# One hybrid encoder layer on one core: the block inverses and the batches behind them written as two streams, and the fill of projections spread evenly

## The chip, the cores and the metric

The kernel runs on one core of one Trainium2 chip. A core has a matrix engine (TensorE, "PE" in the profile, its weight loads "PEld"), three engines for elementwise work (VectorE "DVE", ScalarE "ACT", GpSimd "POOL"), and SyncE ("SP"), which here issues the DMAs. Each engine works through a queue of its own in order, and semaphores make one wait for another. The metric is the time of one execution in microseconds (us) on the device; lower is better.

## The reference

One layer is computed for two groups of frames that share all weights: 64 frames of a running stream and 512 frames of a new one, 576 columns together, with a width of 1024 and 16 heads of 64.

```python
h   = RMSNorm_pre_mix(x)
p   = h @ w_in           # [r|k|v|lora_w|lora_a|lora_g] | [u|v] | gate_A | gate_B
o_A = RWKV-7 time mixing # per token: S = S*w + (S a) b^T + v k^T ;  y = S r
o_B = u * (tril(W_s) LN(v) + b)
m   = sigmoid(gate_A) * (o_A @ w_proj_a) + sigmoid(gate_B) * (o_B @ w_proj_b)
x   = x + RMSNorm_post_mix(m @ w_o)
x   = x + RMSNorm_post_ffn((silu(f @ w_gate) * (f @ w_up)) @ w_down),  f = RMSNorm_pre_ffn(x)
```

The outputs are both groups' `y`, the last projected rows, the states `S`, and the normalised `v` rows of the running stream.

## The kernel before

Activations are kept transposed, with channels on the partitions and 576 columns in two halves of 288. A large product is done in blocks of 128 output channels. Each weight block (512 KB) is loaded into `raw`, split by ScalarE and GpSimd into a high and a low part (`whi`, `wlo`), and multiplied in 48 matmuls (8 pieces of the contraction, 3 products, 2 halves). In the stage in question these matmuls are named `pj`, and `gv` for the gMLP's `v`.

The RWKV stage goes over 8 pairs of heads. The recurrence is done in chunks of 64 tokens, nine per pair, and each chunk needs the inverse of a triangular 64 x 64 matrix. Per pair there are these pieces, each a Python generator:

- `elementwise`: two low-rank products (`z`), the decays (`L`, `EL`), the squared keys `q` and their norms (matmul `n`), then the inner products in the chunks (`am`, giving `AB` and `AK`), three transposes (`tb`), the values (`tv`, `wv`) and a bonus term (`bo`). Its `am` products are marked done by the signal `("A", pair)`, all of it by `("elem", pair)`.
- `inverse`: diagonal 16 x 16 blocks of `AB` go to DRAM (`d_inv`) and come back regrouped as `M`. VectorE inverts them in 15 steps of two instructions (lines 854 and 857, `Xt` and `X`). The result `X` goes to DRAM and comes back as `IV`. VectorE transposes it (`IT<-IV`, line 865), TensorE grows the inverse to 32 and 64 rows in four small products (`m` twice, `mp`, `mu`), with a second transpose between them. Then comes, in the same generator, what is here called the batch: the products `d`, `e` and `c` over all chunks at once, VectorE's sums of them (`TD`, line 944), and `y`.
- `chain`: the state steps over the chunks, one `pc` matmul and one VectorE sum `S` (line 983) each, then the state's part of the output (`py`).
- `finish`: the group norm (`gm`, `gq`), a transpose (`to`), the gate product (`g`), and the store to `d_oa`.

The order of TensorE's instructions is fixed when the program is recorded. A class `Weave` keeps an estimated clock: each generator yields a time or a signal that it waits for, the first ready one in the list records its next instructions, and where none is ready a few matmuls of the next projection block are recorded instead. `LAT` is the table of the estimated waits, and the numbers that `ps1` gets are estimated holds of a PSUM bank. `FILL` says how many blocks of other projections (gates and `u`) are placed behind the three projection blocks (`k`, `r`, `v`) that the next pair needs. Blocks that `FILL` doesn't name run behind the last pair's chain, ahead of the output products `pa`. The other engines' queues are ordered by a scheduler, by its own estimate of when each instruction can run.

One list names all generators in their order of precedence:

```python
clk.run(chain_all(), fin_all(), inv_all(), elem_all(), norm1(0), norm1(1), ...)
```

Of the kernel before, what the change touches and what calls it, by code (L numbers as in the profile page):

```python
# [12 lines left out]
P = 128  # L13
# [7 lines left out]
NPAIR = NH // 2  # L21
# [13 lines left out]
UPR = 0  # L35
F0 = 3
OAE = (0, 0, 0, 0, 0, 0, 0, 0)
FILL = (1, 0, 2, 5, 3, 3, 1, 2)
LAT = {
# [4 lines left out]

# [1 line left out]
}  # L46


# [186 lines left out]
def layer(tc, I, O):  # L235
# [27 lines left out]
    def ps1(name, hold=0.0):  # L263
        clk.take(hold)
        return psum.tile([P, 512], F32, tag="a", bufs=nb["a"], name=name)
# [387 lines left out]
    def elementwise(E):  # L653
# [72 lines left out]
        E["AB"] = AB  # L726
        maskb = mask.unsqueeze(1).broadcast_to([P, 4, P])
        inner = lambda pm, rows_, rows, x, c: mmul(pm[rows_].rearrange("p (a t) -> p a t", t=64), BK[rows, x, c * 64:(c + 1) * 64], AR[rows, :, c * 64:(c + 1) * 64], start=True, stop=True)
        banks = lambda: [ps1("am", 3.0).rearrange("p (j t) -> p j t", t=P) for _ in range(2)]
        yield from clk.free(4)  # L730
        pm = banks()
        for c, j, half_ in PLACES2[:8]:
# [95 lines left out]
        yield LAT["bo0"]  # L828
        for hs in HS:
            yield from clk.free()  # L830
            sb = ps1("bo", 1.2)
            mmul(sb[:, 0:HALF], bonesr, rkh[:, hs], start=True, stop=False)
            mmul(sb[:, 0:HALF], bonesr, rkl[:, hs], start=False, stop=True)
            dve.tensor_tensor(bonus[:, hs], sb[:, 0:HALF], v[:, hs], ALU.mult)
            yield LAT["bo"]
# [2 lines left out]


    def inverse(E):  # L840


        hp_, AB, di = E["hp"], E["AB"], d_inv[E["hp"]]
        M = rp.tile([P, SB, SB], F32, tag="M", name="M")[0:NU]
# [20 lines left out]
        turn = lambda: dve.transpose(IT.rearrange("p c t -> p (c t)"), IV.rearrange("p c t -> p (c t)"))  # L865
        U = AB.rearrange("p j h t -> p (j h) t")
        yield lat("U", hp_)

        PT = rp.tile([P, 10, SB], F32, tag="PT16", name="PT16")
        turn()  # L870
# [31 lines left out]
                mmul(pp[a1:a1 + 32, u], IV[a1:a1 + 32, u, 32:64], PT[a1:a1 + 32, u, :], start=True, stop=True)  # L902
        for _, a1 in blocks:
            act.activation(IT[a1:a1 + 32, :, 0:32], pp[a1:a1 + 32], ACT.Copy)

        yield (("tb", hp_), 0.0)
        yield lat("d0", hp_)
        At, Kt, Vt, AR, AK, WV = (E[n] for n in ("At", "Kt", "Vt", "AR", "AK", "WV"))
        yield from clk.free(3)
        pp = [ps1("d", 2.8).rearrange("p (u t) -> p u t", t=P) for _ in range(3)]  # L910
        for c, b in CROSS:
# [2 lines left out]
                mmul(pp[b][HR[half_], 2 * (j % 2) + h], IT[HR[half2], 2 * j2 + h, :], AB[HR[half2], j2, h, 64:192], start=True, stop=True)  # L914
        for b, rows, j0, j1 in ((0, slice(0, P), 0, 2), (1, slice(0, P), 2, 4), (2, HR[1], 4, 5)):
            act.activation(AB[rows, j0:j1, :, 0:P].rearrange("p j h t -> p (j h) t"), pp[b][rows, 0:2 * (j1 - j0)], ACT.Copy)
        yield LAT["e0"]
        yield (("values", hp_), 0.0)
        if hp_ > 0:
            yield (("chain", hp_ - 1), 0.0)  # L920

# [121 lines left out]
    def elem_all():  # L1043
        for p_ in range(NPAIR):
            if p_ > 0:
                yield (("elem", p_ - 1), 0.0)
            yield from elementwise(EV[p_])
        sp.dma_start(O["shift"], shc)
        e_es.close()
        R["g"], R["gp"] = mk("gmlp")  # L1050
        R["vn"] = [slot(j) for j in range(5)]
        clk.signal("vn")
        R["ln"] = [slot(5 + i) for i in range(2)]
        R["tril"] = R["gp"].tile([P, P], F32, name="tril")
        sp.dma_start(R["tril"], I["cst"][:, NCST:])
        for i in range(2):
            sp.dma_start(R["ln"][i][0:64], I["rows"][i:i + 1, :].broadcast_to([64, D]))

    def inv_all():
        for p_ in range(NPAIR):  # L1060
            yield (("A", p_), 0.0)
            yield from inverse(EV[p_])

    def chain_all():
        for p_ in range(NPAIR):
            yield (("inv", p_), LAT["ch0"])
            yield from chain(EV[p_])

    def fin_all():
        for p_ in range(NPAIR):  # L1070
            yield (("chain", p_), 0.0)
            yield from finish(EV[p_])
# [11 lines left out]
    def oa_all():  # L1084

        yield (("chain", NPAIR - 1), 0.0)
        r_es.close()
        R["m"], R["mp"] = mk("merge")
        raw = []
        wide = lambda n: R["mp"].tile([P, D], F32, tag=n, bufs=1, name=n)  # L1090

        def load(j):
            raw.append(wide(("bias", "wsT")[j - 2])[:, 0:T] if j in (2, 3) else mixed(("gin", "", "zb", "xt")[j // 2], bufs=2))
            sp.dma_start(raw[j], d_oa[j])

        def cut(j):
            keepers(oas, split(R["mp"], raw[j], f"m{j}", eng=(dve, pool)[OAE[j]]))

        for j in range(NPAIR - 1):
            load(j)  # L1100
        yield LAT["oa"]
        for j in range(NPAIR - 1):
            cut(j)
            if j == 3:
                R["bias"], R["wsT"] = wide("bias"), wide("wsT")
                sp.dma_start(R["bias"], I["rows"][2:3, :].broadcast_to([P, D]))
                sp.dma_start(R["wsT"].rearrange("p (g t) -> p g t", t=P), I["wsT"])
            yield LAT["oaj"]
        clk.signal("mp")
        yield (("oa", NPAIR - 1), 0.0)  # L1110
        load(NPAIR - 1)
        yield LAT["oa"]
        cut(NPAIR - 1)
        yield (("behind",), 0.0)
        r2_es.close()
        l_es.close()
        h_es.close()
        R["d0"], R["dp0"] = mk("hidden0", side="right")
        R["x"], R["xf"] = mk("xf", side="right")
        R["f"], R["fp"] = mk("ffnin", side="right")  # L1120
        R["m2"], R["map"] = mk("merge2")
        clk.signal("xf")
# [159 lines left out]
    def norm1(h):  # L1282
        hs = HS[h]
        yield (("po", h), LAT["rs"])
        b = yield from rstd_row(R["fp"], R["acc1"], STARTS[h], "r1")
        keep = tc.keep_in_program_order
        fh, fl = fs
        for j in range(10):
            if j < 8:
                keep(dve.tensor_tensor(y[j][:, hs], y[j][:, hs], b, ALU.mult))  # L1290
            if 1 <= j < 9:
                i = j - 1
                keep(dve.tensor_tensor(y[i][:, hs], y[i][:, hs], xt[i][:, hs], ALU.add))
                act.activation(fh[i][:, hs], y[i][:, hs], ACT.Copy, scale=V("g_pre_ffn", i))
            if j > 1:
                i = j - 2
                keep(dve.scalar_tensor_tensor(fl[i][:, hs], y[i][:, hs], V("g_pre_ffn", i), f(fh[i][:, hs]), ALU.mult, ALU.subtract))
                fcount[h] = i + 1
            yield LAT["f0"] if j == 0 else LAT["f"]
        clk.signal("y", h)  # L1300

    def norm2(h):
        hs = HS[h]
        yield (("y", h), 0.0)
        for j in range(8):
            square_sum(mix_q, R["acc2"], y[j][:, hs], j == 0, hs, pool)
            yield LAT["sq"]
        yield LAT["rs"]
        b = yield from rstd_row(R["fp"], R["acc2"], STARTS[h], "r2")
        act.activation(R["rs2"][:, hs], b, ACT.Copy)  # L1310
        clk.signal("rs2", h)
# [21 lines left out]
    def hidden():  # L1333

        yield (("y", 1), 0.0)
        for h in range(2):
            for j in range(NF):
                yield (("fp", h, j), 0.0)
                yield (("rs2", h), 0.0)
                swiglu(j, {h: halfway[h, j]}, HS[h], pin=True)  # L1340
                clk.signal("d", h, j)
        for j in range(8):
            sp.dma_start(d_x1[j], y[j])
        R["m2"].close()
        R["m"].close()
        R["g"].close()
        R["d"], dp = mk("hidden")
        for j in range(NF, NFF):
            for x, n in zip(ds, "hl"):
                x.append(dp.tile([P, T], F32R, name=f"d{j}{n}"))  # L1350
        clk.signal("hidden")
# [127 lines left out]
    with tc.manual_schedule(engines={mybir.EngineType.PE}):  # L1479
        lora = {0: lora_w(lora_raw(0), pin=False)}  # L1480
        for nm, b in (("k", BLK_K), ("r", BLK_R), ("v", BLK_V)):
            take = Shifted(b, nm, scale=True)
            EV[0][nm] = [take(h, raw0[nm][:, HS[h]]) for h in range(2)][1]
            clk.signal(nm, 0)
        clk.run(chain_all(), fin_all(), inv_all(), elem_all(), norm1(0), norm1(1), norm2(0), norm2(1), hidden(), oa_all(), ob_all(),
                ln_all(), norm3(0), norm3(1))
    R["o"].close()
    R["d0"].close()
# [19 lines left out]
```

## Time and profile before

| | |
|---|---|
| runs shown | 1254.59, 1257.19, 1259.83 us (median 1257.19) |
| profiled execution | 1257.89 us, of which the program's span is 1256.1 |
| mean granted TensorE clock | 0.977 of full speed |
| recurrent stage with its fill | from about 63 us (first `z`) to about 640 us (first `pa`) |

The page of the profile gives the busy time of each engine, then the span in 40 slices, each digit the busy share in tenths. `PEclk` is the clock granted to TensorE, in tenths. The view by stretches gives, for each, its length, the busy time of PE, PEld, DVE, ACT and POOL with the number of instructions, the mean clock, and the share and rate of the DMAs. The view of waits says which engine's instruction waited for which. A row of a time line has start, length, engine, line, operation, output and inputs, shape, count, and in brackets the idle time of the engine ahead of it with what ended it. A row of the chain of work that ended last has start, length and name alone. The trace counts two matmul records for each matmul of full-precision operands, so the counts there are up to twice those of the program.

### The profile page before, as it was taken

How to read it: one execution, taken by the hardware profiler on the slowest of the kernel's cores; microseconds unless marked ns; L12 is line 12 of the kernel's file. 1: busy time of each engine (PE TensorE's matmuls, PEld its weight loads, DVE VectorE, ACT ScalarE, POOL GpSimd, SP SyncE). 2: the span in 40 equal slices, each digit the busy share in tenths (PEclk: the TensorE clock that was granted, in tenths of full speed). 3: DMA queues.
4: the chain of work that ended last, by engine and by line, in shares of the span. 5: the costliest groups of instructions: out<-in, count | busy, mean ns of one | idle time of the engine just before them, and what ended most of it. 6: DMA issues, size and time to landing. Idle time of an engine off the chain costs nothing.

```text
span 1256.1 us, 29917 instructions
## 1 busy us (share of the span) xinstructions
PE 1194.0 (95%) x12926; PEld 1159.7 (92%) x12926; DVE 545.3 (43%) x1081; ACT 464.7 (37%) x889; POOL 621.2 (49%) x484
## 2 busy tenths in 40 slices
PE   6999999998979898889999999899999999999997
PEld 6989999998978898889999999899999999999997
DVE  5756473737364646552803441654333333300003
ACT  5545354544343435333531233443222222222220
POOL 6654454545344544531634554465656556543442
PEclk8989999998989999999999999999999999999998
DMA  5232222222212221221544653232222222243222
GB/s 181 81 97 91 78 87 77 87 78 56 84 49 63 76 76 49 82 74 53 171 161 142 200 156 101 68 110 84 77 80 81 84 85 85 81 156 93 76 77 76
DMA packets 68276, 118.05 MB, mean 94 GB/s; under 512 B 30832, under 2 KB 36208, under 8 KB 68144
## 3 DMA queue, kind: packets, MB, share of 16 engines
q1 hardware_dynamic: 68000, 116.06, 30.0%
q8 instruction: 101, 1.65, 0.5%
q14 instruction: 31, 0.25, 0.1%
q10 hardware_dynamic: 144, 0.08, 0.0%
HBM read 99.83 MB, written 16.28 MB: 92 GB/s over the span
## 4 chain that ended last, share of the span: by engine, by line
PE 75%; DVE 12%; issue 3%; DMA 3%; ACT 3%; POOL 2%; SPq 1%; DVEq 0%; ACTq 0%; POOLq 0%
PE fg L287 20%; PE pj L287 16%; PE po L287 15%; PE pb L287 4%; PE pa L287 4%; PE gv L287 3%; DVE Xt L854 2%; DVE X L857 2%; PE am L287 1%; PE z L287 1%; PE y L287 1%; PE d L287 1%; SPq L862 1%; PE c L287 1%; PE n L287 1%
## 5 line engine op out<-in xcount | busy, mean ns | idle before, releaser
L306 POOL TENSOR_TENSOR wlo<-raw,whi 128x512 fp32r<-128x512 f32 (+1 forms) x288 | 401.7, 1418 | 397.2 <-ACT whi L303 350.1
L303 ACT ACTIVATE whi<-raw 128x1024 fp32r<-128x1024 f32 x144 | 150.2, 1047 | 287.2 <-PE fg L287 174.2
L1259 DVE TENSOR_TENSOR rs<-rs,nsq 128x288 f32<-128x288 f32 (+2 forms) x12 | 9.1, 755 | 106.0 <-ACT nsq L1258 106.0
L1014 POOL TENSOR_TENSOR gm<-gm,mhalf 128x10 f32<-128x10 f32 x8 | 19.6, 2450 | 63.3 <-DVE gm L1013 52.1
L1327 DVE TENSOR_TENSOR ft<-ft,fg 128x288 f32<-128x288 f32 x40 | 16.4, 450 | 68.3 <-PE fg L287 66.8
L1321 DVE TENSOR_TENSOR fg<-fg,rs 128x288 f32<-128x288 f32 x40 | 16.5, 452 | 63.3 <-PE fg L287 63.2
L944 DVE TENSOR_TENSOR TD<-e,AR 64x256 f32<-64x256 f32 x32 | 13.4, 419 | 68.4 <-PE e L287 68.2
L983 DVE TENSOR_TENSOR S<-pc,C 128x64 f32<-128x64 f32 x48 | 10.6, 221 | 66.1 <-PE pc L287 58.6
L854 DVE TENSOR_TENSOR Xt<-X,M 80x15 f32<-80x15 f32 (+7 forms) x120 | 34.7, 290 | 6.9 <-DMA M<-d_inv 3.7
L1324 DVE SCALAR_TENSOR_TENSOR ft<-ft,fg 128x576 f32<-128x576 f32 (+1 forms) x24 | 29.1, 1212 | 18.7 <-ACT ft L1323 18.7
L1325 POOL TENSOR_TENSOR ft<-ft,rs 128x576 f32<-128x576 f32 (+1 forms) x24 | 31.9, 1328 | 7.1 <-DVE ft L1324 7.1
L857 DVE TENSOR_TENSOR X<-X,Xt 80x15 f32<-80x15 f32 (+7 forms) x120 | 30.8, 257 | 3.3
L287 PEld LDWEIGHTS n<-cst,q 128*128 128x128 f32 x80 | 13.2, 252 | 18.1 <-ACT q L685 18.0
L287 PE MATMUL n<-cst,q 128*128 128x2 f32 x80 | 13.7, 297 | 16.8 <-ACT q L685 16.8
L764 POOL TENSOR_TENSOR BK<-BK,EL 128x576 f32<-128x576 f32 x16 | 18.8, 1174 | 22.0 <-PE am L287 22.0
L287 PE MATMUL pj<-h7h,whi 128*128 128x288 f32 x88 | 29.3, 333 | 0.0
L287 PE MATMUL am<-AR,BK 64*64 64x128 f32 x640 | 24.4, 280 | 4.9 <-DVE oo L1034 3.6
L287 PE MATMUL pj<-h1h,whi 128*128 128x288 f32 x88 | 28.7, 326 | 0.0
L287 PE MATMUL pj<-h0h,whi 128*128 128x288 f32 x88 | 28.2, 320 | 0.4 <-ACT st L433 0.4
L287 PE MATMUL pj<-h6h,whi 128*128 128x288 f32 x88 | 28.5, 323 | 0.0
L287 PE MATMUL pj<-h0h,wlo 128*128 128x288 f32 x88 | 26.8, 304 | 1.3 <-POOL wlo L306 1.3
L287 PE MATMUL pj<-h5h,whi 128*128 128x288 f32 x88 | 27.9, 317 | 0.0
(1200 smaller groups left out, 4315.3 us busy)
## 6 DMA issues: line engine op xcount, KB each, us to landing
raw<-in_w_in SPq DMA_DIRECT2D x50, 512.0 KB, 3.7
raw<-in_w_gate SPq DMA_DIRECT2D x22, 512.0 KB, 3.6
raw<-in_w_up SPq DMA_DIRECT2D x22, 512.0 KB, 3.6
raw<-in_w_down SPq DMA_DIRECT2D x16, 512.0 KB, 3.5
raw<-in_w_gv SPq DMA_DIRECT2D x8, 512.0 KB, 3.8
raw<-in_w_proj_a SPq DMA_DIRECT2D x8, 512.0 KB, 4.2
raw<-in_w_proj_b SPq DMA_DIRECT2D x8, 512.0 KB, 3.7
raw<-in_w_o SPq DMA_DIRECT2D x8, 512.0 KB, 3.5
```

The costliest lines, as they stand in the source:

```text
L287: return pe.matmul(out, lhsT, rhs, **kw)
L303: keep(act.activation(hi[:, :cols], raw[:, :cols], ACT.Copy))
L306: keep(pool.tensor_tensor(lo[:, c0:c1], raw[:, c0:c1], f(hi[:, c0:c1]), ALU.subtract))
L764: pool.tensor_tensor(by_chunk(BK[:, x, :]), by_chunk(BK[:, x, :]), EL[:, :, 64:65].broadcast_to([P, NCH, 64]), ALU.mult)
L854: ins = dve.tensor_tensor(t3, X[:, 0:r, s:s + 1].broadcast_to([NU, r, w]), M[:, s:s + 1, s + 1:SB].broadcast_to([NU, r, w]), ALU.mult)
L857: dve.tensor_tensor(X[:, 0:r, s + 1:SB], X[:, 0:r, s + 1:SB], t3, ALU.add)
L944: dve.tensor_tensor(TD[rows, cs, rows], ps[rows, :, 1, :], by_place[rows, cs, 0, :], ALU.add)
L1014: pool.tensor_tensor(m, m, mhalf, ALU.pow)
L1321: keep(dve.tensor_tensor(g[:, HS[h]], pg, rs2[:, HS[h]], ALU.mult))
L1324: keep(dve.scalar_tensor_tensor(t[:, ts], t[:, ts], 1.0, g[:, ts], ALU.add, ALU.mult))
L1325: pool.tensor_tensor(t[:, ts], t[:, ts], rs2[:, ts], ALU.mult)
L1327: dve.tensor_tensor(t[:, HS[h]], t[:, HS[h]], pu, ALU.mult)
```

## The change

The generator `inverse` is cut in two. What is left of it ends with the finished inverse and signals `("it", pair)`. The rest, `d` to `y`, is a generator `batch` of its own, which waits for that signal, and `batch_all` runs it ahead of `inv_all` in the order of precedence. So an inverse may begin when its pair's `am` products are done, and need not wait for the batch of the pair before; its products on TensorE wait for that pair's `d`. `FILL` becomes two blocks a pair and six behind the last pair's, 20 in all in place of 17, so none is left for the place behind the last chain. Some estimates in `LAT` and three holds change.

```diff
-FILL = (1, 0, 2, 5, 3, 3, 1, 2)
+FILL = (2, 2, 2, 2, 2, 2, 2, 6)
...
-"n2": 6.2, "tv": 1.3, "M": 5.5, "U": 20.3, "n2@0": 4.2, "M@0": 3.4
+"n2": 6.8, "tv": 2.2, "M": 6.5, "U": 23.0, "n2@0": 7.5, "M@0": 4.4
...
-        banks = lambda: [ps1("am", 3.0).rearrange("p (j t) -> p j t", t=P) for _ in range(2)]
+        banks = lambda: [ps1("am", 3.6).rearrange("p (j t) -> p j t", t=P) for _ in range(2)]
...
-            sb = ps1("bo", 1.2)
+            sb = ps1("bo", 2.0)
...
     def inverse(E):
...
         yield lat("U", hp_)
+        if hp_ > 0:
+            yield (("d", hp_ - 1), 0.0)
...
             act.activation(IT[a1:a1 + 32, :, 0:32], pp[a1:a1 + 32], ACT.Copy)
-
+        clk.signal("it", hp_)
+
+    def batch(E):
+        hp_ = E["hp"]
+        yield (("it", hp_), 0.0)
         yield (("tb", hp_), 0.0)
         yield lat("d0", hp_)
...
+        clk.signal("d", hp_)
         yield LAT["e0"]
...
+    def batch_all():
+        for p_ in range(NPAIR):
+            yield from batch(EV[p_])
...
-        clk.run(chain_all(), fin_all(), inv_all(), elem_all(), ...
+        clk.run(chain_all(), fin_all(), batch_all(), inv_all(), elem_all(), ...
```

The `LAT` lines are cut to the entries that change.

The first place is on VectorE, where the batch of one pair (`TD`, and `AR` beside it), the chain's state updates (`S`, `So`) and the steps of the next pair's inverse (`Xt`, `X`) meet. Before, at pair 1's batch and pair 2's inverse:

```order
L944 TENSOR_TENSOR TD<-c,AR 64x64 x2
L945 TENSOR_TENSOR AR<-c,AR 128x64
L983 TENSOR_TENSOR S<-pc,C 128x64
L983 TENSOR_TENSOR So<-pc,C 128x64
L983 TENSOR_TENSOR S<-pc,C 128x64 x3
L854 TENSOR_TENSOR Xt<-X,M 80x15
L857 TENSOR_TENSOR X<-X,Xt 80x15
```

Now, at pair 2's batch and the end of pair 3's inverse; pairs 1, 5 and 7 have the same order up to one instruction:

```order
L853 TENSOR_TENSOR Xt<-X,M 80x15
L955 TENSOR_TENSOR TD<-e,AR 64x4x64 x2
L856 TENSOR_TENSOR X<-X,Xt 80x15
L956 TENSOR_TENSOR AR<-e,AR 128x4x64
...
L955 TENSOR_TENSOR TD<-c,AR 64x64 x2
L956 TENSOR_TENSOR AR<-c,AR 128x64
L864 STREAM_TRANSPOSE IT<-IV 128x640
L994 TENSOR_TENSOR S<-pc,C 128x64
L994 TENSOR_TENSOR So<-pc,C 128x64
L994 TENSOR_TENSOR S<-pc,C 128x64 x4
```

The steps of the inverse, which began behind the first state updates, now end ahead of them, and the transpose of the finished blocks stands ahead of the first update too. In pairs 2, 4 and 6 the steps stand between the later updates and the group norm.

The second place is on ScalarE, ahead of the squared keys (`q_..<-k,vec`, line 685) that the key norm `n` of the next pair waits for. Before, pair 2's:

```order
L675 ACTIVATE EL<-L 128x9x64
L677 ACTIVATE sg<-L 128x576
L667 ACTIVATE ta<-z,half 128x288
L485 ACTIVATE shc<-pj 128x1
L486 ACTIVATE q<-pj,vec 128x288
L685 ACTIVATE q_2369<-k,vec 128x576
L687 ACTIVATE aq<-ta,nkk 128x576
```

Now, pair 4's (pairs 2 and 6 alike):

```order
L897 ACTIVATE PT<-mp 32x320 x2
L667 ACTIVATE ta<-z,half 128x288
L675 ACTIVATE EL<-L 128x9x64
L677 ACTIVATE sg<-L 128x576
L1036 ACTIVATE oo<-to,vec 128x448
L687 ACTIVATE aq<-ta,nkk 128x576
L485 ACTIVATE shc<-pj 128x1
L486 ACTIVATE q<-pj,vec 128x288
L1036 ACTIVATE oo<-to,vec 128x128
L685 ACTIVATE q_4419<-k,vec 128x576
```

The evacuation of the inverse's third product (`PT<-mp`), two of the transposed output (`oo<-to`) and the scaled rates (`aq`) now stand ahead of `q`.

More of the change, by code (lines that the diff above doesn't have):

```diff
@@ L904, in inverse @@
             act.activation(IT[a1:a1 + 32, :, 0:32], pp[a1:a1 + 32], ACT.Copy)
+        clk.signal("it", hp_)
+    def batch(E):
+        hp_ = E["hp"]
+        yield (("it", hp_), 0.0)
         yield (("tb", hp_), 0.0)
         yield lat("d0", hp_)
-        At, Kt, Vt, AR, AK, WV = (E[n] for n in ("At", "Kt", "Vt", "AR", "AK", "WV"))
+        AB = E["AB"]
         yield from clk.free(3)
@@ L916, in inverse @@
             act.activation(AB[rows, j0:j1, :, 0:P].rearrange("p j h t -> p (j h) t"), pp[b][rows, 0:2 * (j1 - j0)], ACT.Copy)
+        clk.signal("d", hp_)
         yield LAT["e0"]
         yield (("values", hp_), 0.0)
+        At, Kt, Vt, AR, AK, WV = (E[n] for n in ("At", "Kt", "Vt", "AR", "AK", "WV"))
         if hp_ > 0:
@@ L1484, in layer @@
             clk.signal(nm, 0)
-        clk.run(chain_all(), fin_all(), inv_all(), elem_all(), norm1(0), norm1(1), norm2(0), norm2(1), hidden(), oa_all(), ob_all(),
+        clk.run(chain_all(), fin_all(), batch_all(), inv_all(), elem_all(), norm1(0), norm1(1), norm2(0), norm2(1), hidden(), oa_all(), ob_all(),
                 ln_all(), norm3(0), norm3(1))
```

6 rows, old and new, of the table LAT are left out of this document.

## The prediction

> **What bounds the kernel now.** I read the page first, for the share of each engine and the granted clock by slices.
>
> ```profile
> span 1256.1 us, 29917 instructions
> PE 1194.0 (95%) x12926; PEld 1159.7 (92%) x12926; DVE 545.3 (43%) x1081; ACT 464.7 (37%) x889; POOL 621.2 (49%) x484
> PE   6999999998979898889999999899999999999997
> PEclk8989999998989999999999999999999999999998
> ```
>
> TensorE is busy for 95% of the span, so nothing but its idle time and its slow clock can be won by an order. Both lie in slices 10 to 18, the recurrent stage. The second view is the busy time by stretches: after the start (84 to 300 us), the second half of the recurrent stage, and its end. The column after POOL is the granted clock.
>
> ```profile
> 84.00:300.00 216.00, 212.72 (x3221) 202.64 (x3213) 124.12 (x300) 100.02 (x231) 103.51 (x84) 1.00 0.28 83
> 300.00:560.00 260.00, 231.94 (x3794) 217.66 (x3795) 144.60 (x346) 109.99 (x250) 115.10 (x86) 0.95 0.23 66
> 560.00:640.00 80.00, 77.51 (x963) 74.96 (x963) 33.16 (x65) 34.27 (x62) 32.45 (x24) 0.98 0.40 132
> 300.00:320.00 20.00, 16.40 (x307) 15.36 (x308) 13.71 (x22) 9.06 (x19) 14.80 (x10) 0.83 0.21 58
> 560.00:580.00 20.00, 20.00 (x349) 18.83 (x352) 2.58 (x4) 8.22 (x18) 2.51 (x2) 0.91 0.21 67
> ```
>
> Idle is 3.3 + 28.0 + 2.5 = 33.8 us. The clock costs 260 x 0.05 + 80 x 0.02 = 14.6 us more. So 48.4 us are there to be won. The two lower rows price one drop: 20 x 0.17 = 3.4 us after a long wait, 20 x 0.09 = 1.8 us after a short one. Third, who ended TensorE's waits between 84 and 640 us (total, times, longest):
>
> ```profile
> PE n L287 <- ACT q L685: 13.7, 4, 5.9
> PE pc L287 <- DVE S L983: 4.1, 7, 1.1
> PE am L287 <- DVE oo L1034: 3.6, 2, 2.8
> PE wv L287 <- ACT Vt L802: 2.4, 2, 1.2
> PE m L287 <- DVE IT L865: 2.1, 1, 2.1
> ```
>
> Most of it is the key norm `n`, which waits for the squared keys `q` from ScalarE. Fourth, VectorE's time line in pair 4 tells why:
>
> ```profile
> 356.59 0.18 DVE L857 TENSOR_TENSOR X<-X,Xt 80x15 f32<-80x15 f32 x1
> 364.14 0.84 DVE L865 STREAM_TRANSPOSE IT<-IV 128x640 f32<-128x640 f32 x1 [4.18 <-DMA IV<-d_inv]
> 365.80 1.35 DVE L671 TENSOR_TENSOR_SCAN L<-rmask,sg 128x576 f32<-128x576 f32 x1
> ```
>
> VectorE stood 4.18 us at the transpose of the inverse, whose DMAs had not landed. The decay scan `L` of the next pair stood behind it, and `q` stands behind `EL<-L` on ScalarE. What stalls TensorE is a transpose at the head of VectorE's in-order queue, ahead of work that did not need it.
>
> **The change part by part.** *TensorE's work* is the same 10,235 matrix instructions in another order: 0 us. *The fill* moves three projection blocks from behind the last pair to ahead of it, also 0 us by itself. *The old waits* go: an inverse now starts as soon as its own elementwise part is done, some 40 us ahead of its first matmul, so the `n` waits of pairs 3 to 5 lose their cause. I credit the whole 48.4 us, which is the most there is, and charge what comes new. *The DMAs* are the same eighteen of an inverse (eight stores from `AB`, the load of `M`, the store of `X`, eight loads of `IV`), moved on SyncE's queue ahead of or behind one or two weight loads that wait for nothing late: 0 us, inside the bounds below. GpSimd's instructions are the same and keep their places relative to the projections.
>
> *The new wait.* In pairs 1, 3, 5 and 7 the changed order puts all the steps of the inverse ahead of `TD`, and the transpose `IT` ahead of the first state update `S` of the pair before. `S` feeds the next state step `pc` on TensorE. So I need when `IT` can run and when TensorE asks for `S`, both counted from the first `am` matmul of the inverse's pair. Chain and time lines of pairs 0 and 2:
>
> ```profile
> 83.37 1.10 PE am L287 x32
> 91.19 1.84 DMA M<-d_inv
> 93.12 0.59 DVE L854 TENSOR_TENSOR Xt<-X,M 80x15 f32<-80x15 f32 x1 [3.68 <-DMA M<-d_inv]
> 93.95 0.18 DVE L854 TENSOR_TENSOR Xt<-X,M 80x28 f32<-80x28 f32 x1
> 95.32 0.21 DVE L854 TENSOR_TENSOR Xt<-X,M 80x55 f32<-80x55 f32 x1
> 100.46 0.68 DVE L783 TENSOR_TENSOR AB<-tb,rn 128x512 f32<-128x512 f32 x1
> 103.44 0.18 DVE L857 TENSOR_TENSOR X<-X,Xt 80x15 f32<-80x15 f32 x1
> 112.11 0.84 DVE L865 STREAM_TRANSPOSE IT<-IV 128x640 f32<-128x640 f32 x1 [3.32 <-DMA IV<-d_inv]
> 191.64 1.88 PE L287 MATMUL am<-AR,BK 64*64 64x128 f32 x48
> 200.63 0.32 SPq L845 DMA_DIRECT2D M<-d_inv  x1
> ```
>
> From `am` to the first step of the inverse: 93.12 - 83.37 = 9.75 us in pair 0. In pair 2 the load of `M` was issued 9.0 us after `am`, plus 1.84 us to land: 10.9. I take 11.1, as pair 2 is like those that follow. The 30 steps took 93.12 to 103.62, 10.5 us, of which 0.95 us were two `AB` operations that now stand elsewhere: 9.55. Six undisturbed ones took 95.32 - 93.95 = 1.37 us, so 30 take 6.9 at least, and 7.4 with the first, long one. I take 8.6, between the two. From the last step to `IT`: 112.11 - 103.62 = 8.5 us in pair 0, 364.14 - 356.77 = 7.4 in pair 4; I take 7.5. `IT` itself 0.84, `S` 0.2. Sum: 11.1 + 8.6 + 7.5 + 0.84 + 0.2 = 28.2 us (between 25.6 and 31).
>
> TensorE meanwhile, by these rows of pair 2 (chain and time line):
>
> ```profile
> 196.05 1.03 PE am L287 x32
> 206.60 3.79 PE pj L287 x27
> 199.21 1.60 PE L287 MATMUL d<-AB,IT 64*64 64x128 f32 x36
> 212.88 0.33 PE L287 MATMUL pc<-S,TD 128*128 128x64 f32 x2
> ```
>
> From `d` to the second state step: 13.7 us, with the same blocks between them in both orders. From `am` to `d` the new order has two `am` groups (1.7 and 1.0), 36 projection matmuls at 3.79 / 27 = 0.14 (5.0), and one `mu` (0.8): 8.5. TensorE asks for `S` at 22.2 us and gets it at 28.2: a wait of 6.0 us, between 3.4 and 8.8. A wait of that length lowers the clock: 3.4 us more. That is 9.4 us in each of four pairs, 37.6 us. In pairs 2, 4 and 6 the steps stand between the `S` updates, which are due earlier, and I charge nothing there.
>
> *The key norm behind an odd pair* (`n` of pairs 2, 4, 6). Before, in pair 2:
>
> ```profile
> 171.65 0.29 PE L287 MATMUL z<-dwr,lwh 128*128 128x288 f32 x1
> 179.03 0.78 ACT L685 ACTIVATE q<-k,vec 128x576 f32<-128x576 f32 x1
> ```
>
> `q` was ready 8.2 us after the first `z`. Now ScalarE has two `PT`, two `oo` and one `aq` more ahead of `q`, some 2.9 us by their own rows, of which its idle time in that stretch takes 1.2: 9.9 us. TensorE's new order has 7.5 us of work from `z` to `n` (33 projection matmuls 4.4, `z` 1.1, `mp` and `mu` with their switches 1.6, `to` 0.4). The wait is 2.4 us at most by this and 0.7 at least. I take 2.1, and 1.7 for the clock: 3.8 x 3 = 11.4 us.
>
> [...]
>
> *The key norm behind an even pair* (pairs 3, 5, 7): `IT` is still ahead of `k` and `L`. By the new order the steps end with the group norm, which I put at 24 us after `am`; 7.5 and 0.84 more make about 33, and `k`, `oo`, `L` and ScalarE's part some 9 to 10 us more. TensorE's blocks reach `n` at 42. I charge 0.8 us each, 2.4 in all, with 0 and 2.5 each as bounds. *Short waits* for `S` of about 1 us, 4.1 in all, I leave as they are.
>
> *The end.* Two blocks fewer now lie between the last gate `g` and `pa`. Before, SyncE's queue held the first load for `pa` behind the last output's round trip:
>
> ```profile
> 619.15 0.29 PE L287 MATMUL g<-dgh,lgh 128*128 128x288 f32 x1
> 626.34 0.33 SPq L1036 DMA_DIRECT2D d_oa<-oo  x1
> 631.57 0.33 SPq L1094 DMA_DIRECT2D xt<-d_oa  x1
> 632.95 0.38 SPq L296 DMA_DIRECT2D raw<-in_w_proj_a  x1
> 635.25 0.76 DVE L348 TENSOR_TENSOR m7l<-xt,m7h 128x576 fp32r<-128x576 f32 x1 [7.36 <-ACT m7h L347]
> ```
>
> Three of these loads now stand ahead of that store, so the weights are there in time. The last output was split (`m7l`) 16.9 us after `g`; it is needed behind 87 `gv` and 126 `pa` matmuls, 213 x 0.12 to 0.14 = 26 to 30 us after `g`. 0 us, and 3 us as the bound if that cover is too short.
>
> **Sum.** -48.4 + 37.6 + 11.4 + 2.4 + 4.1 = +7.1 us. Against the profiled execution's own 1257.89 us (span 1256.1, and 1257.19 the median of the runs) that is 1265 us.
>
> **Rivals.** *The new wait is short.* With 25.6 us instead of 28.2, `S` is 3.4 us late, with 1.8 us of clock, 20.8 us in four pairs; if `q` is in time too, the sum is -48.4 + 20.8 + 4.1 = -23.5: 1234 us. For it: the 9.75 us of pair 0 and the 7.4 of pair 4 are such ends. Against it: no pair had all of them. It decides for faster by 0.5% once the wait with its clock is under 6 us a pair, all else as charged. *The waits cancel.* With `S` 5 us late (8.4 with the clock, 33.6 in all) and the even `n` 2.1 us late without a drop (6.3), it comes to 1256. *The clock does not follow.* If waits of 6 us cost no clock, 4 x 3.4 + 3 x 1.7 = 18.7 us fall away: 1246. [...] The row of 300 to 320 us, behind a wait of 3.7 us, speaks against it. *The waits are longer.* With 8.8 us at `S` (12.2 with the clock, 48.8 in all), 2.4 + 3.4 at each even `n` (17.4), 2.5 at each odd one (7.5), and 3 at the end: 1290.
>
> **Numbers.** The forecast as sized (1254 to 1278 us) has a chance of 0.50, the short wait 0.22, the cancelling 0.13, the steady clock 0.05, the longer waits 0.10. The range of 1238 to 1282 us leaves out about half of the short and half of the long case. A change within 0.5% (6.3 us) is about what a measurement of this kernel can't tell from none. Slower by more has the longer waits and three quarters of the forecast, 0.46; the same has the cancelling and the forecast's rest, 0.27; faster the other two, 0.27.
>
> **What would show it.** In the changed profile: waits of `pc` on `S` near 6 us in four pairs, each with VectorE standing at `IT` for the DMA of `IV`, and a lower clock behind each. Waits of `n` on `q` near 2 us in pairs 2, 4 and 6, none near 6. No wait of `am` on `oo`. If VectorE's idle time ahead of `IT` is under 1 us in the odd pairs, the landing time is what I have wrong, and the kernel is faster. If `pc` waits but the clock stays at 1.00, it is the price of the drop.

## The result and the profile after

| | before | after |
|---|---|---|
| median of four runs (us) | 1257.28 (1254.59 to 1259.83) | 1271.40 (1264.63 to 1275.67) |
| ratio, 95% interval | | 1.0108 (1.0058 to 1.0157) |
| profiled execution, span | 1257.89, 1256.1 | 1264.63, 1262.8 |
| mean granted clock | 0.977 | 0.966 |

The change made the kernel 1.1% slower, 14 us in the medians; 1265 us was forecast, between 1238 and 1282. The profiled execution was the shortest of the four; why is told under the experiments. The page of after, first lines, busy time and slices:

```profile
span 1262.8 us, 29911 instructions
PE 1200.6 (95%) x12926; PEld 1166.8 (92%) x12926; DVE 539.3 (43%) x1081; ACT 464.4 (37%) x889; POOL 614.8 (49%) x484
PE   7999999989999899989999999989999999999997
PEclk9999898998998989889999999989999999999998
```

The share of TensorE is the same 95%. What changed is where the clock is below full: before, behind the start, in slices 10 to 18, now from slice 5 on. The view by stretches, the same three as before:

```profile
84.00:300.00 216.00, 202.44 (x2963) 192.10 (x2962) 113.75 (x281) 90.87 (x207) 95.46 (x77) 0.93 0.26 76
300.00:560.00 260.00, 239.92 (x3770) 226.56 (x3767) 140.22 (x340) 112.76 (x260) 114.56 (x89) 0.94 0.25 71
560.00:640.00 80.00, 78.26 (x1107) 75.92 (x1107) 28.42 (x57) 32.70 (x66) 26.23 (x20) 0.97 0.36 115
```

The first 216 us had 3.3 us of idle time and a clock of 1.00 before; now 13.6 us and 0.93. Who ended the waits, from 84 us to the first `pa`:

```profile
PE n L287 <- ACT q L685: 10.4, 6, 2.6
PE pc L287 <- DVE So L994: 9.9, 3, 4.0
PE pc L287 <- ACT C L959: 8.8, 4, 3.5
PE z L287 <- DVE bonus L834: 3.8, 3, 1.5
```

The waits of `am` on `oo`, of `wv` on `Vt` and of `m` on `IT`, and the `n` waits of 3.7 to 5.9 us are gone. New are waits of the state steps, in two forms. VectorE's time line in pair 3 (first and last rows) shows both; rows of TensorE, ScalarE and SyncE stand behind it:

```profile
269.78 0.17 DVE L853 TENSOR_TENSOR Xt<-X,M 80x15 f32<-80x15 f32 x1 [3.23 <-DMA M<-d_inv]
278.51 0.85 DVE L955 TENSOR_TENSOR TD<-e,AR 64x256 f32<-64x256 f32 x2
281.60 0.23 DVE L956 TENSOR_TENSOR AR<-c,AR 128x64 f32<-128x64 f32 x1
288.60 0.84 DVE L864 STREAM_TRANSPOSE IT<-IV 128x640 f32<-128x640 f32 x1 [6.77 <-DMA X<-in_cst]
289.37 0.18 DVE L994 TENSOR_TENSOR S<-pc,C 128x64 f32<-128x64 f32 x1
```

```profile
272.63 1.10 PE L287 MATMUL e<-AB,At 64*64 64x128 f32 x32
281.29 3.88 SPq L861 DMA_DIRECT2D IV<-d_inv  x8
281.92 0.44 ACT L959 ACTIVATE C<-c 128x320 f32<-128x320 f32 x1 [6.79 <-DVE AR L956]
282.41 0.69 PE L287 MATMUL pc<-C,TD 128*128 128x64 f32 x2 [3.51 <-ACT C L959]
289.74 0.69 PE L287 MATMUL pc<-S,TD 128*128 128x64 f32 x2 [2.32 <-DVE So L994]
```

The thirty steps of the inverse run from 269.8 us on and hold `TD` until 278.5, though its input `e` ended at 273.7: TensorE's first state step waits 3.5 us. Its row names `C`, ScalarE's copy, and by ScalarE's row `C` in turn had waited for `AR`, which stands behind `TD` on VectorE. Then VectorE stands 6.8 us at the transpose whose DMAs have not landed, `S` is behind it, and TensorE waits 2.3 us more. (The row of `IT` names the load of `X` for the next pair, which landed last of all; the last of the transpose's own eight loads landed 0.2 us earlier in the trace.) SyncE takes 3.9 us to issue the eight loads, one behind another; no run here makes that shorter.

### The profile page after: what moved, and what is told of

Read it like the earlier page. It is cut to its first block, busy times and chain, and to the rows that moved or that the text cites. A ratio compares the mean times of both kernels' runs of the same rounds, so it can differ in the third digit from the quotient of the medians.

```text
span 1262.8 us, 29911 instructions
## 1 busy us (share of the span) xinstructions
PE 1200.6 (95%) x12926; PEld 1166.8 (92%) x12926; DVE 539.3 (43%) x1081; ACT 464.4 (37%) x889; POOL 614.8 (49%) x484
## 4 chain that ended last, share of the span: by engine, by line
PE 70%; DVE 11%; ACT 5%; issue 5%; DMA 4%; SPq 3%; POOL 2%; DVEq 0%; ACTq 0%; POOLq 0%
PE fg L287 20%; PE po L287 14%; PE pj L287 11%; PE gv L287 5%; PE pb L287 4%; PE pa L287 3%; SPq L861 2%; DVE X L856 1%; DVE Xt L853 1%; POOL wlo L306 1%; PE fp L287 1%; PE z L287 1%; SPq L748 1%; PE n L287 1%; PE am L287 1%
## 5 line engine op out<-in xcount | busy, mean ns | idle before, releaser
L306 POOL TENSOR_TENSOR wlo<-raw,whi 128x512 fp32r<-128x512 f32 (+1 forms) x288 | 397.0, 1400 | 408.7 <-ACT whi L303 377.4
L789 POOL TENSOR_TENSOR AR<-eye,eC 128x576 f32<-128x576 f32 x8 | 9.4, 1177 | 63.8 <-PE tr L291 63.8
L853 DVE TENSOR_TENSOR Xt<-X,M 80x15 f32<-80x15 f32 (+7 forms) x120 | 31.0, 258 | 20.1 <-DMA M<-d_inv 16.6
L864 DVE STREAM_TRANSPOSE IT<-IV 128x640 f32<-128x640 f32 x16 | 13.5, 845 | 55.0 <-DMA IV<-d_inv 32.0
L1339 DVE SCALAR_TENSOR_TENSOR ft<-ft,fg 128x576 f32<-128x576 f32 (+1 forms) x24 | 28.6, 1190 | 19.0 <-ACT ft L1338 19.0
L287 PE MATMUL pc<-S,TD 128*128 128x64 f32 x112 | 21.6, 278 | 9.9 <-DVE So L994 9.9
L287 PEld LDWEIGHTS pc<-S,TD 128*128 128x128 f32 x112 | 19.6, 210 | 11.4 <-DVE So L994 10.8
L431 ACT ACTIVATE st<-pj 128x288 f32<-128x288 f32 x30 | 12.2, 407 | 48.0 <-PE pj L287 47.4
L287 PE MATMUL pj<-h0h,whi 128*128 128x288 f32 x88 | 29.5, 336 | 0.0
L287 PE MATMUL pj<-h2h,whi 128*128 128x288 f32 x88 | 29.1, 331 | 0.0
L287 PE MATMUL pj<-h3h,whi 128*128 128x288 f32 x88 | 28.4, 323 | 0.0
L287 PE MATMUL pj<-h4h,whi 128*128 128x288 f32 x88 | 28.3, 322 | 0.0
```

What stands on the lines that cost most here:

```text
L287: return pe.matmul(out, lhsT, rhs, **kw)
L306: keep(pool.tensor_tensor(lo[:, c0:c1], raw[:, c0:c1], f(hi[:, c0:c1]), ALU.subtract))
L853: ins = dve.tensor_tensor(t3, X[:, 0:r, s:s + 1].broadcast_to([NU, r, w]), M[:, s:s + 1, s + 1:SB].broadcast_to([NU, r, w]), ALU.mult)
L1339: keep(dve.scalar_tensor_tensor(t[:, ts], t[:, ts], 1.0, g[:, ts], ALU.add, ALU.mult))
```

## The experiments

All kernels compute the full layer. The edits to VectorE's and ScalarE's order use two means: `keep_in_program_order`, which keeps one instruction behind everything written ahead of it, and the point where it is written. "Idle" and "clock" below are worked out from each trace between 84 us and the first `pa`: TensorE's gaps, and half of its busy time in stretches at half clock. One execution each, so a difference of 3 us says little, and the execution isn't always near the median: it took 1261.8 us with the new fill in the kernel before, 1240.4 with `IT` kept there, and 1244.3 with `n` later. The ratios stand against runs of the kernel before on the same chip.

| kernel | median us | ratio to before (95%) | idle | clock |
|---|---|---|---|---|
| before | 1257.3 | | 33.8 | 14.0 |
| after | 1271.4 | 1.0108 (1.0058 to 1.0157) | 35.9 | 29.8 |
| after, again | 1271.3 | 1.0110 (1.0075 to 1.0145) | 38.1 | 28.6 |
| `IT` kept | 1251.4 | 0.9949 (0.9926 to 0.9973) | 22.5 | 24.2 |
| and steps behind `TD` | 1243.1 | 0.9891 (0.9863 to 0.9918) | 16.8 | 20.1 |
| after, old fill | 1278.0 | 1.0167 (1.0143 to 1.0191) | 44.3 | 30.4 |
| before, new fill | 1254.9 | 0.9989 (0.9963 to 1.0015) | 31.3 | 24.7 |
| before, `IT` kept | 1246.2 | 0.9924 (0.9901 to 0.9948) | 29.0 | 9.9 |
| before, `n` twice | 1276.3 | 1.0162 (1.0131 to 1.0192) | 36.8 | 28.1 |
| before, full filler | 1263.3 | 1.0043 (1.0017 to 1.0070) | 34.2 | 15.3 |
| steps kernel, `n` later | 1237.7 | 0.9858 (0.9812 to 0.9904) | 20.8 | 15.3 |
| `S` ahead of the steps | 1249.3 | 0.9946 (0.9927 to 0.9965) | 24.4 | 21.6 |
| that, `q` first | 1247.1 | 0.9923 (0.9895 to 0.9952) | 21.8 | 24.8 |
| steps kernel, `q` first | 1234.8 | 0.9792 (0.9739 to 0.9844) | 16.3 | 15.0 |

**The transpose ahead of the state updates.** One edit to the changed kernel:

```diff
-        turn()
+        tc.keep_in_program_order(turn())
```

> The changed kernel with one edit: the first transpose IT of each inverse keeps its place in the written order on VectorE, so it stands behind the state updates S in pairs 1, 3, 5, 7 and behind bonus, k and the decay scan L in pairs 2, 4, 6. TensorE's, ScalarE's, GpSimd's and SyncE's orders are unchanged, row for row. Theory (a transpose that waits for its DMAs holds VectorE's queue): the waits of pc on So (9.9 us), of z on bonus (3.8) and of n on q in pairs 3, 5, 7 (3.8) go, and with them some 11 to 13 us of half clock; the waits of pc on C (8.8) and of n in pairs 2, 4, 6 (6.7) stay. About 28 us less than the changed kernel's 1271.4: 1243 us (1235 to 1252). Rival (the wait only moves: the inverse's matmuls m now wait for the later transpose): 1262 to 1273 us, with new waits of m on IT. Second rival (S is late because of C, not because of IT): the waits on S stay near 3 us a pair, and only z and the odd n go: 1258 to 1264 us.

It took 1251.4 us, 20 us less. Its waits from 84 us to the first `pa`:

```profile
PE pc L287 <- ACT C L959: 8.4, 4, 3.5
PE n L287 <- ACT q L685: 6.7, 3, 2.6
PE m L287 <- issue: 3.3, 3, 1.6
PE m L287 <- DVE IT L864: 1.2, 5, 0.2
```

The waits on `So` and `bonus` and the `n` waits of pairs 3, 5, 7 are gone, and `m` waits 0.2 us at most for the later transpose: both rivals fall. Idle time fell by 13.4 us, where 17.5 was expected, as waits of `m` with no releaser in the profile came up; the clock's share fell by 5.6 us where 11 to 13 was expected.

**The steps ahead of `TD`.** Besides, the thirty steps become a stream of their own, which in the odd pairs starts 10 us behind the signal `A` in place of 6.5 (the new stream alone):

```diff
+    def steps_all():
+        for p_ in range(NPAIR):
+            yield (("A", p_), lat("X", p_))
+            steps_of_inverse(EV[p_])
```

> The same edit as in the kernel with IT kept in its place, and also: in pairs 1, 3, 5, 7 the thirty steps of the inverse are written 3.5 us later, so that they stand behind TD and AR on VectorE. TensorE's order is the same. Theory (the steps ahead of TD make the state chain start late): the waits of pc on C (8.8 us in four pairs) go too, with some 6 to 8 us of clock: 15 us less than with IT kept alone, 1228 us (1218 to 1238). Rival (C is late for ScalarE's sake or for e itself): the waits on C stay, 1240 to 1248 us. Second rival (the inverse is now late for its own matmuls): waits of m on IT of 2 us or more in the odd pairs, and 1245 us or more.

1243.1 us, 8 less. That is in the first rival's range, but the waits are not the rival's:

```profile
PE n L287 <- ACT q L685: 6.7, 3, 2.6
PE pc L287 <- DVE So L1002: 4.3, 2, 2.4
PE m L287 <- issue: 2.2, 2, 1.4
```

The waits on `C` are gone, so it was the steps ahead of `TD` that made them. But 4.3 us came back at `S` in pairs 5 and 7, where steps now stand between `TD` and `S`; that is more than half of the 7 us that were missing from the expected 15. With TensorE's order untouched, two moves on VectorE took 28 us from the changed kernel, twice what the change had lost.

**The fill alone**, both ways round (only the line `FILL` is exchanged).

> The changed kernel with the old table of the fill (1, 0, 2, 5, 3, 3, 1, 2 blocks behind the pairs), all else as changed. Theory (the fill by itself is worth nothing, the loss is in VectorE's order): 1262 to 1277 us, with waits of pc on C and So in the odd pairs as in the changed kernel. Rival (the new fill makes the loss, since pairs with less fill have less to cover their waits): 1257 us or less, and the waits in the odd pairs go.

> The kernel before with the new table of the fill (2 blocks behind each pair and 6 behind the last), and nothing else of the change. Theory (the fill by itself is worth nothing): 1251 to 1263 us. If half of the loss is the fill's, 1264 us or more; if the new fill is a gain that the two streams ate up, 1245 us or less.

In the kernel before, the new fill is worth nothing (0.9963 to 1.0015), as the prediction had it. In the changed kernel it is worth 6.6 us (1278.0 us without it, just above the theory's range): with the old one the waits of `pc` on `C` and `So` were 14.6 and 12.5 us. They grew in pairs 1 and 7 (6.6 and 10 us in place of 3.0 and 5.0), around which the old table has fewer blocks (1 and 0, 1 and 2, in place of 2 and 2, 2 and 6), and not in pairs 3 and 5, where it has as many or more.

```profile
PE pc L287 <- ACT C L959: 14.6, 4, 7.0
PE pc L287 <- DVE So L994: 12.5, 4, 3.9
```

So the fill did not make the loss; it made it smaller.

**What lowers the clock.** The waits were about as long as forecast, but the clock cost 1.6 times as much (29.8 us for 18.7). These two kernels add TensorE work to the kernel before, and nothing to wait for. The first issues the products of `n`, of 2 columns each, twice; the second has eight full matmuls there, whose results are not used (the new matmuls alone):

```diff
+        for j in range(5):
+            pe.matmul(s[:, j, :], q2[:, START2[j]:START2[j] + P], bones[:, 0:P:64], start=True, stop=True)
```

```diff
...
+        for j in range(8):
+            pe.matmul(pn2[:, 16:16 + HALF], bonesr, dgh[:, 0:HALF], start=True, stop=True)
```

> The kernel before, with the ten matrix passes of each key norm n issued twice (the same values written again): about 1.14 us more of tiny work (2 columns each) in each of eight pairs, 9.1 us in all, and nothing to wait for. Theory (the granted clock falls when the array is little used for some 2 us of a 3.4 us window, and n and m count as unused like waiting does): new stretches at half clock at n in pairs 1, 2 and 3, where before has none, 4 to 10 us on top: 1270 to 1277 us. Rival (only idle time counts): 1257 + 9 = 1266 us, as with the heavy filler, and no new stretches in the first 300 us. Second rival (TensorE's work hides in its waits): under 1262.

> The kernel before, with eight full matmuls of 288 columns (0.134 us each, 1.07 us) behind each key norm n, 8.6 us in all: as much time as the doubled n, but with the array in full use. By the first theory: no new stretches at half clock, or fewer than before, 1262 to 1267 us, and 4 us or more below the doubled n. By the rival that only idle time counts: within 3 us of the doubled n.

1276.3 and 1263.3 us: about equal time added (9.1 and 8.6 us, as estimated ahead of the runs), 13 us apart, which the clock accounts for (28.1 against 15.3; idle 36.8 against 34.2). First the kernel with `n` twice at pair 1's `n`, three rows of TensorE and two stretches of one window each:

```profile
118.46 0.82 PE L287 MATMUL m<-IV,PT 32*16 32x16 f32 x80
119.21 1.28 PE L287 MATMUL n<-cst,q 128*128 128x2 f32 x10
120.35 1.76 PE L698 MATMUL n<-cst,q 128*128 128x2 f32 x10
```

```profile
117.50:120.91 3.41, 3.41 (x104) 3.22 (x103) 2.55 (x3) 1.62 (x5) 2.18 (x2) 1.00 0.38 142
120.92:124.33 3.41, 3.41 (x17) 3.41 (x17) 1.19 (x4) 0.54 (x3) 1.69 (x1) 0.50 0.00 0
```

The kernel with the full filler at the same place:

```profile
117.79:121.20 3.41, 3.41 (x103) 3.22 (x102) 3.14 (x3) 1.18 (x4) 1.59 (x2) 1.00 0.30 113
121.21:124.61 3.40, 3.40 (x57) 3.23 (x56) 2.36 (x5) 1.51 (x3) 2.73 (x2) 1.00 0.00 0
```

TensorE did not idle for a moment in either first window, and yet the clock was halved behind the one that held 1.7 us of `n` (2 columns each) and 0.75 us of `m` (16 columns each). A window is 3.413 us here by the traces: in before and in after the stretches at half clock start whole multiples of 3.413 us apart, and those of the recurrent stage last one to four times that (3.41 to 13.65 us). By these rows the clock fell behind a window that was not idle at all. Between 84 us and the first `pa`, in all 14 traces here, each of the 44 full-speed windows with 2.0 us or more of idle time was followed by half clock; windows with `n` or `m` in them were followed by it with less or none (1.1 us in pair 5 of after, none in the row of 117.50 us). What exactly the clock goes by (columns, matmuls or their size) these runs don't show.

**The kernel before with `IT` kept**, the same one-line edit.

> The kernel before, with one stream and the old fill, and one edit: the first transpose IT of each inverse keeps its written place on VectorE, behind the scan L. TensorE's order is that of before, row for row. Theory (what stalled before is the same thing as after, a transpose that waits for its DMAs ahead of work that did not need it): the waits of n on q in pairs 4 to 7 (13.7 us) go, with three stretches of 6.8 us at half clock, 8 to 9 us: from 1257 to 1235 us (1228 to 1245). Then the two streams are not needed for the gain. Rival (the inverse's matmuls m, which come some 12 us after the transpose here, are now late): waits of m on IT of 2 us or more a pair, and 1250 us or more.

1246.2 us: the `n` waits of 13.7 us fell to 4.7, but `m` waited 3.5 us for `IT` in pair 7 and `am` 3.0 us for the later `AR`.

```profile
PE n L287 <- ACT q L685: 4.7, 4, 1.9
PE m L287 <- DVE IT L865: 3.5, 1, 3.5
PE am L287 <- DVE AR L720: 3.0, 2, 1.5
```

So the transpose was the cause of most of the old `n` waits too, and both theory and rival have a part: the time lies between the two. The two streams with the transpose and the steps in order took 1243.1 us, 3 us less, and the intervals of the two ratios overlap. What is gained on ScalarE below was not tried on one stream, so how much the two streams are worth by themselves stays open.

**The key norms of pairs 2, 4 and 6.** Four kernels. First, `n` asked for later (`"n2@2"`, `"n2@4"`, `"n2@6"`: 9.4 in place of 6.8):

> The kernel with IT kept and the steps behind TD, and besides: the key norms n of pairs 2, 4 and 6 are asked for 2.6 us later in TensorE's written order, with projection blocks ahead of them. Theory (these n wait 6.7 us in all for q from ScalarE, and each wait has a stretch of 6.8 us at half clock behind it): both go, 6.7 + 9 = some 15 us, so from 1243.1 to 1228 us (1220 to 1236). Rival (the norm is then late for am, or another wait takes its place): 1239 us or more, with waits of am on rn's users or of n still there.

1237.7 us, between theory and rival: 5.4 us less where 15 was expected. These `n` waits went, and the clock's share fell by 5 us, but TensorE's order moved from there on, and `am` waited for `AR` (3.8 us), `m` for `IT` (3.9 us) and `pa` (2.8 us). In the profiled execution, the slowest of the four, idle time rose by 4.0 us in all.

Next, the steps written 15 us behind `A` in the odd pairs, and ScalarE's copies `IT<-mu` kept in place, which puts `q` ahead of them; then `aq` kept in place too:

> The kernel with IT kept and the steps behind TD, and two more moves with TensorE's order as it was: the steps of pairs 1, 3, 5, 7 are written another 5 us later, so that the first state updates S are ahead of them on VectorE, and ScalarE's copies IT<-mu keep their written place, which puts q ahead of them in pairs 2, 4, 6. Theory: the waits of pc on So (4.3 us in pairs 5 and 7) go with some 2 us of clock, and the waits of n in pairs 2, 4, 6 fall from 6.7 to about 4 us: 8 to 11 us less than 1243: 1233 us (1228 to 1239). Rival (later steps make the inverse late): waits of m on IT of 1 us or more in the odd pairs, 1241 us or more.

> As the kernel with S ahead of the steps, and also ScalarE's aq keeps its written place, behind q: q is some 1.7 us earlier than with IT<-mu alone behind it. Theory: the waits of n in pairs 2, 4, 6 are under 1 us each and the half clock behind them goes in at least two of the three: 1226 us (1220 to 1233), 4 to 9 us under the kernel without this. Rival (aq is needed by GpSimd and VectorE for BK, and the next am waits for it, or n still finds its window little used): no faster than that kernel within 3 us.

The rivals won: 1249.3 and 1247.1 us. The waits of the first of the two:

```profile
PE pc L287 <- DVE S L1002: 6.9, 4, 3.5
PE m L287 <- DVE IT L876: 6.8, 7, 3.2
PE n L287 <- ACT q L685: 5.7, 3, 2.1
```

Steps that stand between the updates make `S` late in turn, and the inverse is late for `m`, by 1.9 us in pair 3 and 3.2 in pair 5. The steps have a narrow place: ahead of `TD` 8.4 us were waited at `C`, with the steps among the `S` updates 6.8 us at `m` and 6.9 at `S`, with them just behind `TD` 4.3 us at `So`. So the last kernel keeps them there and has only ScalarE's two moves:

> The kernel with IT kept and the steps just behind TD (1243.1 us), and on ScalarE aq and the copies IT<-mu keep their written place, behind q. TensorE's order is as changed, row for row. Theory (the n waits of pairs 2, 4, 6 are ScalarE's order, 2.0 to 2.6 us each, and a shorter wait may leave its window over the bound of the clock): n waits 0.8 to 1.3 us each there, no waits of m on IT over 0.5 us since the steps stay early, 3 us less of waiting and 3 us of clock: 1237 us (1232 to 1241). Rival (the later aq makes BK and the next am late): 1242 us or more, with waits of am on BK.

1234.8 us, some 2% under before (the four runs took 1223.6 to 1235.8) and 36.6 us under the change; 8 us came from ScalarE's order alone. Its waits:

```profile
PE m L287 <- issue: 4.7, 3, 1.7
PE n L287 <- ACT q L685: 3.4, 3, 1.3
PE pc L287 <- DVE So L1002: 2.5, 2, 2.0
```

**The changed kernel again.**

> The changed kernel itself once more, for its spread. Its profiled execution took 1264.6 us, the other three 1271.3 to 1275.7. Theory (the difference is the rhythm of the gate and up projections of the last stage, 1920 matmuls that ran 130.3 ns apart in that profile and 133.5 ns in the one of before; 3.2 ns x 1920 = 6.2 us): a median of 1268 to 1274 us; if the profile shows 133.5 ns, its span is 1268 to 1271 us with the first pa still at 651 to 654 us. Rival (the recurrent stage itself varies between executions): pa starts 3 us or more later or earlier than 652.5.

The gate matmuls `fg` of the last stage, one row each of before, after, and after again:

```profile
L287 PE MATMUL fg<-f0h,whi x80: 292/295/399, 844.8 to 1096.4; 128*128 128x288 f32 x80
...
L287 PE MATMUL fg<-f0h,whi x80: 290/292/398, 858.6 to 1103.2; 128*128 128x288 f32 x80
...
L287 PE MATMUL fg<-f0h,whi x80: 292/300/402, 861.2 to 1112.1; 128*128 128x288 f32 x80
```

From first to last these took 251.6, 244.6 and 250.9 us, with the same 1874 of the stage's 1920 matmuls between them at full clock: on average 133.5, 130.3 and 133.5 ns apart, without one gap of 1.6, 0.7 and 0.9 us. In that stage the first profiled execution of the change won 7.0 us that are not the change's. That explains why the profiles stand 6.7 us apart and the medians 14. But the first `pa` was 3.5 us later as well (656.0 for 652.5), so the recurrent stage also varies between executions, as the rival said.

## Why the prediction was right, and where it was off

The forecast case came true: old waits gone, new ones at `S` and `n`, and a sum on the slow side. By its own steps:

- *The old waits* (48.4 us credited). Right: by the table before had 33.8 + 14.0 = 47.8, and none of its five kinds is left in that form. But the prediction put the long `n` waits in pairs 3 to 5; by the trace of before they are those of pairs 4, 5 and 6 (3.7, 5.9 and 3.7 us).
- *The new wait of the odd pairs* (6.0 + 3.4 us each, 37.6). Near in size, and the landing was right: `IT` was to start 27.2 us behind `am`, and started 28.7, 29.5, 26.6 and 26.6 behind it. TensorE was to ask for `S` at 22.2 us; in pairs 5 and 7 it would have asked at 22.8, without its wait one step earlier. The waits were 3.0, 5.8, 5.0 and 5.0 us, 18.8 in all for 24, and the stretches at half clock behind them cost 14.8 for 13.6. What I had not seen is that half of it comes one step earlier: `TD` behind the steps already holds the first state step. In pair 1 that was all of it. So keeping `IT` in its place took away the waits on `So` alone, and the wait on `C` needed an edit of its own.
- *`n` of pairs 2, 4, 6* (2.1 + 1.7 each, 11.4). The waits were 2.0, 2.1 and 2.6 us; the clock cost 8.4 for 5.1, as two of the three stretches were 6.8 us long.
- *`n` of pairs 3, 5, 7* (0.8 each, no clock, 2.4). This is the term that failed. The waits were 0.7, 1.5 and 1.5 us, inside the bounds, but behind the last two came stretches of 6.8 us: 6.6 us of clock where I had written none. I priced the clock by the length of a wait; the kernels with `n` twice and with the filler show that idle time alone does not set it: the clock fell behind a window with none, 2.45 us of it `n` and `m`. In pair 5 a wait of 1.1 us inside a window with 0.9 us of `m` was enough, in pair 7 one of 1.5 us with 1.0 us of `n`; in pair 3 a wait of 0.7 us with 0.8 us of `n` was not.

```profile
384.32:391.14 6.82, 6.44 (x103) 6.13 (x104) 2.42 (x5) 1.88 (x7) 3.25 (x2) 0.50 0.15 56
520.85:527.67 6.82, 6.82 (x105) 6.50 (x105) 3.44 (x8) 2.68 (x7) 2.88 (x2) 0.50 0.01 3
```

- *`z` behind `bonus`* was not in the sum: 3.8 us, no clock. `bonus` stands behind the same transpose in the even pairs, which I had followed for `k` and `L` only:

```profile
239.12 0.84 DVE L864 STREAM_TRANSPOSE IT<-IV 128x640 f32<-128x640 f32 x1 [4.69 <-DMA IV<-d_inv]
239.89 0.78 DVE L834 TENSOR_TENSOR bonus<-bo,v 128x288 f32<-128x288 f32 x2
```

- *Short waits for `S`* (4.1): none were left, since `S` now follows a longer wait.
- *The fill* (0): right in the old order, a gain of 6.6 us in the new one. *The end* (0): right, `pa` waited 0.5 us as before.

Waiting came to 35.9 us where the terms say 36.8, the clock to 29.8 where they say 18.7. So the waits were right as a sum, in part by luck: the state steps were 5.2 us under and `S` 4.1, while `z` (3.8 us), the longer `n` waits (1.7) and four small waits that no term had (2.7 together) made up for most of it. The clock was 11 us short. By this account the change cost some 18 us more than it won. The first `pa` came 13.0 us later: at 84 us the new order was some 2 us ahead in its matmuls, and some 3 us I cannot place. That the forecast of 1265 met the profiled execution (1264.6) is luck, made by the 7 us of the last stage; against the median it was 6.4 us low.

Of the rivals, the cancelling waits came nearest: they had 33.6 us at the state steps, clock included, and the runs show 18.8 + 14.8 = 33.6. What they left out is the half clock behind the `n` waits, 15 us. The short wait fell with the landing times. The steady clock fell most clearly. The waits of 2 us were not free either: each of the three (2.0, 2.1 and 2.6 us) was followed by half clock.

## What to carry to other kernels

When work is started earlier, look at what its instructions are now ahead of on each in-order queue: an instruction that waits for a DMA should stand behind everything on its engine that is due before the DMA can land, by landing times from the trace. Price the clock by windows, not by waits: here a window with 0.9 us of tiny matmuls (`m`) and a wait of 1.1 us was followed by half clock, and one with 0.8 us of them (`n`) and 0.7 us of waiting was not. Look for the narrow place of a block of work from both sides, since both "too early" and "too late" cost here.

## What the runs showed of the hardware

- In the kernel with `n` twice the clock was 0.50 behind a window in which TensorE never idled, busy for 3.41 of 3.41 us (rows above, 117.50 to 124.33 us).
- The same matmuls at full clock ran in two rhythms, 130.3 or 133.5 ns apart over 1920 of them, in 4 and 10 of the 14 profiled executions here. Nothing in the rows tells why; it stays open.
- Steps of the inverse took some 1.2 us in place of 0.2 while GpSimd made `wlo`. In the changed kernel's trace 12 of the 240 steps took over 1 us, all of them then. VectorE, then GpSimd, in pair 3:

```profile
274.09 0.22 DVE L853 TENSOR_TENSOR Xt<-X,M 80x60 f32<-80x60 f32 x1
274.34 1.17 DVE L856 TENSOR_TENSOR X<-X,Xt 80x60 f32<-80x60 f32 x1
275.55 1.21 DVE L853 TENSOR_TENSOR Xt<-X,M 80x55 f32<-80x55 f32 x1
```

```profile
274.17 2.51 POOL L306 TENSOR_TENSOR wlo<-raw,whi 128x512 fp32r<-128x512 f32 x2 [6.23 <-ACT whi L303]
```

Each of the two slow steps here, 1.17 and 1.21 us, took about the time of one of the two `wlo` in GpSimd's row (2.51 us for both). What holds them the rows don't show. In pair 5 of the kernel with the steps behind `TD` such a pair of slow steps stands ahead of the first `S`, which TensorE waited 2.4 us for.
